# Moving the gathered expert sums from VectorE to GpSimd, half of them into the way down, with three smaller moves

## The chip, the cores and the metric

The kernel runs on one NeuronCore of a Trainium2 chip. Five engines work side by side, each through its own queue, in order: TensorE (PE; its weight loads are listed apart as PEld), VectorE (DVE), ScalarE (ACT), GpSimd (POOL) and SyncE (SP), which only issues DMAs. ACT and POOL issue DMAs too. The metric is device microseconds (us) of one execution; lower is better.

## The reference

Two transformer-like blocks on 512 tokens of width 1024, in float32. What the change touches is the PEER layer of the first block and the S5 layer of the second. PEER scores 128 x 128 product keys, keeps 16 of 16,384 experts in each of 8 heads for every token, and sums the chosen experts, each of which is one row of `expert_down` and one of `expert_up`:

```
u = expert_down[ib]                                  # the way down
act = gelu(einsum("td,thkd->thk", hb, u))
v = expert_up[ib]                                    # the way up
out = einsum("thk,thkd->td", gb * act, v)
```

S5 is a grouped, complex, diagonal state space layer: per group a product into the state, a scan over time, a product out of it, then gelu and two products (GLU) over all channels.

## The kernel before, in words

The tokens stand in the columns of a matrix, channels in the partitions. A product is made of three matmuls (`mm3`, L126 to L128): weights are split into `hi` (ACT, L118) and `lo` (DVE, L119), activations likewise, and hi by hi, hi by lo and lo by hi are added up. Weights come as 128x1024 tiles by SP's queue into `raw`; `raw`, `hi` and `lo` have three buffers each.

PEER treats 416 tokens (TD) densely: all 16,384 experts, 128 at a time, j = 0 to 127. The way down multiplies each tile of `expert_down` with all these tokens, takes gelu, and writes pairs of j as `act_d` (L823 to L825). Beside it, `select` finds the 16 best, and `scatter` writes the gates of the 416 tokens as a dense matrix `g_d` (one-hot matmuls at L745; the DMA to DRAM at L749 is issued by POOL). The way up reads `act_d` (tile `aj`) and, for eight j at a time, `g_d` (tile `gt`) by ACT's queue, multiplies them to `wg` (DVE, L1077), splits `wg` to `wh` (ACT) and `wl` (DVE), and adds up with the tiles of `expert_up` in eight PSUM banks.

The other 96 tokens (TG) go by gathers: 64 tokens on two partitions each and 32 on four (`GROUPS`), in 64 + 32 gathers of 128 rows. POOL issues each as an indirect DMA (L756) into one of three `row` buffers. For `expert_down`, DVE forms the dot products with the tokens (`dot`, L764); for `expert_up`, DVE adds gate x row to `tsum` (`add`, L777 for the first and L779). There are 96 dots and 96 sums; 16 of the sums (`NOW`) stand on the way down, 80 on the way up. 16 PE matmuls per group fold `tsum` into the result (L1097).

What fills the time beside the dense experts is a list of closures with a cost each (`fill`): every j takes as many as its share `per` allows. A scheduler with a timeline of its own then sets the order in each engine's queue; `soon()` raises the priority of the loads, splits and `wg`, and `issue_after` keeps an instruction behind another one.

On the way up the list also holds the preparation of S5's matrices (`s5_prepare`; its input `s5in` is loaded from j = 3 on; results go to DRAM as `mats_d`, by POOL's queue). In the S5 stage later, `u_proj` writes u to DRAM and reads it back in another shape as `u4` (eight DMAs for each of eight m, L1397), `tables(m)` builds the matrices of four pairs (L1406 to L1434), `carry(gi)` the states (L1444 on), `answer(gi)` the outputs (L1478 on). In between stand the products `gate_proj`, `u_proj` and `gla_out` (moving operand `A` for the first two, `B` for the last). Gelu of S5's output then feeds GLU, again with moving operand `A`.

Of the kernel before, what the change touches and what calls it, by code (L numbers as in the profile page):

```python
# [7 lines left out]
F32 = mybir.dt.float32  # L8
# [51 lines left out]
def tile_blocks(ctx, tc, I, out):  # L60
# [500 lines left out]
    with tc.tile_pool(name="peert", bufs=2, reuse_waits="tile") as pt, tc.tile_pool(name="peer", bufs=1, reuse_waits="tile") as pe:  # L561
# [210 lines left out]
        def add(g, i):  # L772
            raw = fetch(I["eu"], g, i)
            w = ggate[g][:, i : i + 1]
            if i == 0:
                tsum[g] = gx.tile([P, D], F32, tag=f"tok{g}", name=f"tsum{g}")
                nc.vector.tensor_scalar(tsum[g], raw, w, None, ALU.mult)  # L777
            else:
                nc.vector.scalar_tensor_tensor(tsum[g], raw, w, tsum[g], ALU.mult, ALU.add)  # L779

        def later(fn):
            with tc.issue_after(low[0].ins):
                fn()

        dot_of = lambda p: (1.4, lambda p=p: dot(*p))
        adds = [(1.3, lambda p=p: later(lambda: add(*p))) for p in picks]


        SPILL, NOW = 0, 16
# [8 lines left out]
        dotted = []  # L798
        for g, (_, n, _) in enumerate(GROUPS):
            dotted += [dot_of(p) for p in picks if p[0] == g]  # L800
            dotted.append((0.1, lambda g=g: weigh(g)))
        cut = len(dotted) - SPILL - 1 if SPILL else len(dotted)
        down, left = dotted[:cut], dotted[cut:]
        down += adds[:NOW]
# [9 lines left out]
        fill.extend(down)  # L814

        per = sum(c for c, _ in fill) / (P - 8)
        done[0] = 0.0
        for j in range(P):
            ps = psum("w")
            linear(ps, I["ed"][j], (hh, hl), TD, TG)  # L820
            if j % 2 == 0:
                at_ = px.tile([P, 2, TD], F32, tag="act", name=nm("at_"))
            nc.scalar.activation(at_[:, j % 2], ps[:, :TD], AF.Gelu)  # L823
            if j % 2 == 1:
                nc.scalar.dma_start(act_d[j // 2], at_.rearrange("p a t -> p (a t)"))  # L825
            run_fill(min((j + 1) * per - done[0], 4.2))
# [199 lines left out]
    with tc.tile_pool(name="s5p", bufs=1, reuse_waits="tile") as s5p, tc.tile_pool(name="up", bufs=2, reuse_waits="tile") as pu:  # L1026
# [6 lines left out]
        def beside():  # L1033
# [7 lines left out]
            of_first = GROUPS[0][1]  # L1041
            gathers = []
            for i, a in enumerate(adds[NOW:of_first]):
                gathers.append(a)
                if left and i % 2 == 1:
                    gathers.append(left.pop(0))
            gathers += left + adds[max(of_first, NOW) :]
# [325 lines left out]
    with tc.tile_pool(name="s5a", bufs=2, reuse_waits="tile") as sp:  # L1373
# [7 lines left out]
        def u_proj(m):  # L1381
# [352 lines left out]
```

## Time and profile before

| | |
|---|---|
| time, median of 3 runs | 2742.34 us (2730.85 to 2746.29) |
| the profiled execution's own time | 2736.44 us |
| span of its profile | 2734.7 us |
| PE busy | 2630.8 us, 96% |
| DVE / ACT / POOL busy | 1874.4 (69%) / 1070.8 (39%) / 491.1 us (18%) |
| the way down ends, the way up begins | about 1103 us, 1107 us |
| the way up's last matmuls, S5's last answer | about 1728 us, 2200 us |

The span is what lies between the first and the last instruction; 1.7 us lie around it. PE's busy share counts modelled matmul ends, so whether a stretch is full is read from how many matmuls it holds. Where PE waits, the profile names the engine that released it. A DMA-issuing instruction stands under the queue's name (SPq, ACTq) and takes no engine time, save on POOL, which makes the descriptors itself.

### The profile page before, as it was taken

To read this page: it belongs to the slowest core of one execution; us is meant where nothing else is said; L and a number is where in the kernel's file an instruction comes from. 1 tells how busy PE (TensorE), PEld (TensorE's weight loads), DVE (VectorE), ACT (ScalarE), POOL (GpSimd) and SP (SyncE) were. 2 spreads that over 40 slices of the span, in tenths; PEclk is the share of its full clock that TensorE was granted. 3 is DMA by queue.
4 is the path that set the end of the run, shared out by engine and by line. 5 is a ranking of instruction groups with operands and counts; after the bars stand their busy time and mean duration, and the time that the engine had idled before them with its cause. 6 is when DMAs were issued, how large, how long until landed. Compare 5 with 4: busy or idle time off the path is not lost.

```text
span 2734.7 us, 36390 instructions
## 1 busy us (share of the span) xinstructions
PE 2630.8 (96%) x13784; PEld 2349.5 (86%) x13784; DVE 1874.4 (69%) x3430; ACT 1070.8 (39%) x1510; POOL 491.1 (18%) x431
## 2 busy tenths in 40 slices
PE   6999999999999999999999899999999989999997
PEld 5777789999999999999899899877788878688886
DVE  5777699998998874788688576744456654562543
ACT  4564333434445444334433233544323243432221
POOL 0001000343343021224423120100002320010100
PEclk9999999999999999999999999999999999999999
DMA  6324424889888577979887887222265654233321
GB/s 255 101 87 139 144 93 133 282 286 327 301 307 323 188 263 259 313 273 339 297 319 265 281 302 258 82 63 70 70 193 177 191 159 132 72 98 96 97 96 66
DMA packets 182304, 532.95 MB, mean 195 GB/s; under 512 B 20592, under 2 KB 59472, under 8 KB 180208
## 3 DMA queue, kind: packets, MB, share of 16 engines
q1 hardware_dynamic: 89872, 282.57, 31.2%
q0 software_dynamic: 39952, 157.64, 16.5%
q10 hardware_dynamic: 52304, 90.41, 9.7%
q8 instruction: 108, 1.77, 0.3%
q14 instruction: 68, 0.56, 0.1%
HBM read 448.98 MB, written 80.41 MB: 194 GB/s over the span
## 4 chain that ended last, share of the span: by engine, by line
PE 84%; DMA 6%; DVE 5%; issue 2%; ACT 2%; POOL 1%; ACTq 0%; SPq 0%; DVEq 0%; POOLq 0%
PE ps L127 24%; PE ps L126 24%; PE ps L128 24%; PE ps L745 4%; DMA gt<-g_d 3%; DMA row<-in_eu_dram,gid 1%; DVE lo L119 1%; PE ps L1307 1%; PE ps L1310 1%; DVE wg L1077 1%; PE ps L615 1%; PE ps L148 0%; PE ps L1421 0%; ACT hi L118 0%; PE ps L487 0%
## 5 line engine op out<-in xcount | busy, mean ns | idle before, releaser
L118 ACT ACTIVATE hi<-raw 128x1024 fp32r<-128x1024 f32 (+2 forms) x459 | 481.3, 1051 | 1068.0 <-PE ps L127 796.9
L119 DVE TENSOR_TENSOR lo<-raw,hi 128x1024 fp32r<-128x1024 f32 (+2 forms) x459 | 579.4, 1264 | 347.6 <-ACT hi L118 319.1
L126 PE MATMUL ps<-h2h,hi 128*128 128x416 f32 (+1 forms) x1152 | 413.1, 360 | 3.9 <-ACT h2h L569 3.0
L127 PE MATMUL ps<-h2l,hi 128*128 128x416 f32 (+1 forms) x1152 | 413.1, 359 | 2.9 <-DVE h2l L570 2.9
L128 PE MATMUL ps<-h2h,lo 128*128 128x416 f32 (+1 forms) x1152 | 411.2, 358 | 0.0
L127 PE MATMUL ps<-wl,hi 128*128 128x416 f32 x1024 | 363.8, 355 | 11.4 <-DVE wl L132 11.4
L128 PE MATMUL ps<-wh,lo 128*128 128x416 f32 x1024 | 358.4, 357 | 10.9 <-DVE lo L119 10.9
L126 PE MATMUL ps<-wh,hi 128*128 128x416 f32 x1024 | 351.2, 355 | 6.6 <-ACT wh L131 4.5
L126 PE MATMUL ps<-Ah,hi 128*128 128x512 f32 (+2 forms) x944 | 337.7, 363 | 18.0 <-ACT Ah L131 7.0
L127 PE MATMUL ps<-Al,hi 128*128 128x512 f32 (+2 forms) x944 | 340.6, 361 | 2.7 <-DVE Al L1123 2.7
L128 PE MATMUL ps<-Ah,lo 128*128 128x512 f32 (+2 forms) x944 | 338.1, 359 | 0.5 <-DVE lo L119 0.5
L756 POOL DMA_INDIRECT row<-in_eu_dram,gid x96 | 181.9, 1895 | 398.5 <-DVE tsum L779 329.6
L126 PEld LDWEIGHTS ps<-h2h,hi 128*128 128x128 f32 x1152 | 218.0, 189 | 11.5 <-ACT h2h L569 3.8
L127 PEld LDWEIGHTS ps<-h2l,hi 128*128 128x128 f32 x1152 | 217.8, 189 | 9.9 <-DVE h2l L570 3.6
L128 PEld LDWEIGHTS ps<-h2h,lo 128*128 128x128 f32 x1152 | 217.8, 189 | 6.4
L126 PEld LDWEIGHTS ps<-Ah,hi 128*128 128x128 f32 x944 | 179.0, 191 | 50.0 <-ACT Ah L131 7.9
L127 PEld LDWEIGHTS ps<-wl,hi 128*128 128x128 f32 x1024 | 194.4, 190 | 16.6 <-DVE wl L132 13.0
L127 PEld LDWEIGHTS ps<-Al,hi 128*128 128x128 f32 x944 | 180.2, 191 | 32.6 <-issue 5.0
L128 PEld LDWEIGHTS ps<-wh,lo 128*128 128x128 f32 x1024 | 195.5, 191 | 13.1 <-DVE lo L119 11.9
L128 PEld LDWEIGHTS ps<-Ah,lo 128*128 128x128 f32 x944 | 179.6, 190 | 30.7 <-issue 6.0
L126 PEld LDWEIGHTS ps<-wh,hi 128*128 128x128 f32 x1024 | 196.0, 192 | 10.2 <-ACT wh L131 5.2
L756 POOL DMA_INDIRECT row<-in_ed_r_dram,gid x96 | 144.6, 1506 | 218.9 <-DVE dots L764 194.1
(602 smaller groups left out, 4199.5 us busy)
## 6 DMA issues: line engine op xcount, KB each, us to landing
raw<-in_ed_dram SPq DMA_DIRECT2D x128, 512.0 KB, 5.1
raw<-in_eu_dram SPq DMA_DIRECT2D x128, 512.0 KB, 5.5
raw<-in_win_dram SPq DMA_DIRECT2D x67, 512.0 KB, 3.6
raw<-in_wff_dram SPq DMA_DIRECT2D x64, 512.0 KB, 3.8
g_d<-gst POOLq DMA_DIRECT2D x13, 2048.0 KB, 9.7
aj<-act_d ACTq DMA_DIRECT2D x64, 416.0 KB, 4.5
wa<-in_wada_dram SPq DMA_DIRECT2D x46, 512.0 KB, 4.5
gt<-g_d ACTq DMA_DIRECT2D x45, 512.0 KB, 9.8
```

Of the source, the lines that this page charges most:

```text
L118: top[0] = nc.scalar.activation(hi[:, :n], raw[:, :n], AF.Copy)
L119: low[0] = nc.vector.tensor_sub(lo[:, :n], raw[:, :n], hi[:, :n].bitcast(F32))
L126: nc.tensor.matmul(ps, wh, x[0], start=first, stop=False)
L127: nc.tensor.matmul(ps, wh, x[1], start=False, stop=False)
L128: nc.tensor.matmul(ps, wl, x[0], start=False, stop=last)
L615: nc.tensor.matmul(ps[:, t * P : t * P + P], q[:, t * P : t * P + P], skt[:, m], start=True, stop=True)
L745: nc.tensor.matmul(ps[:, i * P : i * P + P], o1[:, c, :, i], o2[a][:, c, :, i], start=a == 0, stop=a == 1)
L756: nc.gpsimd.indirect_dma_start(out=raw, out_offset=None, in_=src.rearrange("a b d -> (a b) d"), in_offset=bass.IndirectOffsetOnAxis(ap=gid ...
L1077: nc.vector.tensor_tensor(wg.rearrange("p (c t) -> p c t", t=TC), aj[:, j % 2].rearrange("p (c t) -> p c t", t=TC), gt[:, :, j % 8], ALU.mult)
L1307: nc.tensor.matmul(po[hs], qx[:, c * 64 : c * 64 + 64], st, start=False, stop=True)
L1310: nc.tensor.matmul(ps, kt[hs, j], vt[hs, j], start=True, stop=True)
```

## The change

Four edits. First, all 96 sums move from DVE to POOL. A sum is now two instructions, gate x row in place (`tensor_scalar`, with the first one of a group writing `tsum`) and `tsum` + row (`tensor_tensor`). They are issued one gather behind on the way down (lag 1) and two behind on the way up. 48 sums instead of 16 are in the way down's list: 32 in turn with the 32 dots of the second group, 16 at the list's end. Second, `aj` for j = 0 and 1 goes to two buffers of another tag, by SP's queue, and `gt` is issued behind `hi` of j - 8 instead of j - 6. Third, the read-back of `u4` is issued by POOL instead of SP. Fourth, `tables(m + 1)` is written behind `carry(gi + 1)` instead of ahead of it.

```diff
-        def add(g, i):
-            raw = fetch(I["eu"], g, i)
-            w = ggate[g][:, i : i + 1]
-            if i == 0:
-                tsum[g] = gx.tile([P, D], F32, tag=f"tok{g}", name=f"tsum{g}")
-                nc.vector.tensor_scalar(tsum[g], raw, w, None, ALU.mult)
-            else:
-                nc.vector.scalar_tensor_tensor(tsum[g], raw, w, tsum[g], ALU.mult, ALU.add)
+        pending = []
+        def sums_of(lag):
+            while len(pending) > lag:
+                g, i, raw = pending.pop(0)
+                w = ggate[g][:, i : i + 1]
+                if g not in tsum:
+                    tsum[g] = gx.tile([P, D], F32, tag=f"tok{g}", name=f"tsum{g}")
+                    nc.gpsimd.tensor_scalar(tsum[g], raw, w, None, ALU.mult)
+                else:
+                    nc.gpsimd.tensor_scalar(raw, raw, w, None, ALU.mult)
+                    nc.gpsimd.tensor_tensor(tsum[g], tsum[g], raw, ALU.add)
+        def add(g, i, lag):
+            pending.append((g, i, fetch(I["eu"], g, i)))
+            sums_of(lag)
...
-        SPILL, NOW = 0, 16
+        NOW, LAST = 48, 16
...
+        down = [dot_of(p) for p in picks[:n0]] + [(0.1, lambda: weigh(0))]
+        dots_, adds_ = [dot_of(p) for p in picks[n0:]], adds[: NOW - LAST]
+        while dots_ or adds_:
+            for l in (dots_, adds_):
+                if l:
+                    down.append(l.pop(0))
...
-        fill.extend(down)
-        per = sum(c for c, _ in fill) / (P - 8)
+        fill.extend(down + adds[NOW - LAST : NOW] + [(0.1, lambda: sums_of(0))])
+        per = sum(c for c, _ in fill) / (P - 6)
...
-            run_fill(min((j + 1) * per - done[0], 4.2))
+            run_fill(min((j + 1) * per - done[0], 4.8))
...
-                with tc.issue_after(tops[max(j - 6, 0)].ins) if j else ExitStack():
+                with tc.issue_after(tops[max(j - 8, 0)].ins) if j else ExitStack():
...
+                if j == 0:
+                    aj = [tp.tile([P, TD], F32, tag="tl", name=nm("aj"), bufs=3) for _ in range(2)]
+                    for i, a in enumerate(aj):
+                        nc.sync.dma_start(a, act_d[0][:, i * TD : i * TD + TD])
...
-                        nc.sync.dma_start(u4[r0 : r0 + 16, 4 * m : 4 * m + 4], usrc[g, s])
+                        nc.gpsimd.dma_start(u4[r0 : r0 + 16, 4 * m : 4 * m + 4], usrc[g, s])
...
-            if gi % 2 == 0 and gi + 2 < NGR:
-                nxt = tables(gi // 2 + 1)
             if gi % 2 == 1:
                 sts = nxt
             cur, held = held, carry(gi + 1, sts) if gi + 1 < NGR else None
+            if gi % 2 == 0 and gi + 2 < NGR:
+                nxt = tables(gi // 2 + 1)
```

POOL's queue in the middle of the way down, at the first gathers of the second group (`gid_2365`; `in_ed_r` rows are for dots, `in_eu` rows for sums). Before:

```order
L756 DMA row_7204<-in_ed_r_dram,gid_2361 128x1024
L756 DMA row_7243<-in_ed_r_dram,gid_2365 128x1024
L756 DMA row_7309<-in_ed_r_dram,gid_2365 128x1024
L756 DMA row_7407<-in_ed_r_dram,gid_2365 128x1024
L756 DMA row_7411<-in_ed_r_dram,gid_2365 128x1024
```

Now:

```order
L756 DMA row_6770<-in_ed_r_dram,gid_2365 128x1024
L756 DMA row_6869<-in_eu_dram,gid_2361 128x1024
L756 DMA row_6871<-in_ed_r_dram,gid_2365 128x1024
L756 DMA row_6937<-in_eu_dram,gid_2361 128x1024
L781 TENSOR_SCALAR tsum_6939<-row_6869,ggate_2362 128x1024
L783 TENSOR_SCALAR row_6937<-row_6937,ggate_2362 128x1024
L756 DMA row_7002<-in_ed_r_dram,gid_2365 128x1024
L756 DMA row_7039<-in_eu_dram,gid_2361 128x1024
L784 TENSOR_TENSOR tsum_6939<-tsum_6939,row_6937 128x1024
L756 DMA row_7104<-in_ed_r_dram,gid_2365 128x1024
L783 TENSOR_SCALAR row_7039<-row_7039,ggate_2362 128x1024
```

Each gather for a dot now has a gather for a sum and the two instructions of an earlier sum around it in the same queue. Later in this queue 34 of the 48 sums stand ahead of the two memsets of S5's preparation (L957), and the other 14 behind them and behind the DMA `mats_d<-s5in`, which waits for an input that is loaded on the way up.

The issue of one `gt` on ACT and its first use on DVE, at j = 98 of the way up. Before, ACT and then DVE:

```order
L118 ACTIVATE hi_14288<-raw_14287 128x1024
L1067 DMA gt_14528<-g_d 128x4x256
L119 TENSOR_TENSOR lo_14289<-raw_14287,hi_14288 128x1024
L132 TENSOR_TENSOR wl_14295<-wg_14293,wh_14294 128x416
L119 TENSOR_TENSOR lo_14325<-raw_14323,hi_14324 128x1024
L779 SCALAR_TENSOR_TENSOR tsum_13340<-row_14359,ggate_2366,tsum_13340 128x1024
L132 TENSOR_TENSOR wl_14331<-wg_14329,wh_14330 128x416
L1077 TENSOR_TENSOR wg_14541<-aj_14533,gt_14528 128x416
```

Now, at j = 96, ACT and then DVE:

```order
L118 ACTIVATE hi_14321<-raw_14320 128x1024
L1068 DMA gt_14626<-g_d 128x4x256
L119 TENSOR_TENSOR lo_14322<-raw_14320,hi_14321 128x1024
L132 TENSOR_TENSOR wl_14328<-wg_14326,wh_14327 128x416
L119 TENSOR_TENSOR lo_14358<-raw_14356,hi_14357 128x1024
L132 TENSOR_TENSOR wl_14364<-wg_14362,wh_14363 128x416
L1084 TENSOR_TENSOR wg_14639<-aj_14631,gt_14626 128x416
```

The issue moved two j ahead, and the first `wg` that reads the tile moved with it: in both one further `lo` lies between.

PE's queue at S5's last answer. Before:

```order
L1480 MATMUL ps_19546<-s5xi_19537,em_19426 128x128
L126 MATMUL ps_19969<-Ah_19633,hi_19971 128x512
L126 MATMUL ps_20005<-Ah_19633,hi_20007 128x512
L126 MATMUL ps_20043<-Ah_19633,hi_20045 128x512
L127 MATMUL ps_19969<-Al_19634,hi_19971 128x512
```

Now:

```order
L1487 MATMUL ps_19642<-s5xi_19633,em_19522 128x128
L128 MATMUL ps_19781<-Bh_15648,lo_19784 128x512
L126 MATMUL ps_19781<-Bh_15648,hi_19783 128x512
L127 MATMUL ps_19781<-Bl_15649,hi_19783 128x512
L128 MATMUL ps_19781<-Bh_15648,lo_19784 128x512
```

Before, GLU (`Ah_19633`, made by gelu from S5's output) came right behind the last answer; now 175 matmuls of `gla_out` (`Bh_15648`) come first. In exchange 417 instead of 489 of the three-matmul products stand between the first carry and the last answer; the first two answers have few between them.

## Rows read from the trace of the kernel before

**Rows 1.** Windows: length; busy PE, PEld, DVE, ACT, POOL (instructions); clock, DMA share, GB/s.

```profile
500.00:1050.00 550.00, 549.13 (x3213) 530.71 (x3212) 476.63 (x736) 256.32 (x318) 175.99 (x123) 1.00 0.82 288
1100.00:1150.00 50.00, 45.68 (x231) 44.73 (x230) 36.26 (x93) 17.88 (x25) 11.05 (x5) 0.93 0.91 307
1150.00:1700.00 550.00, 525.38 (x2727) 515.64 (x2726) 425.48 (x677) 190.57 (x260) 163.75 (x92) 0.98 0.86 296
1250.00:1300.00 50.00, 50.00 (x267) 49.46 (x266) 43.28 (x59) 21.51 (x30) 24.74 (x12) 1.00 0.97 348
1500.00:1600.00 100.00, 88.38 (x449) 85.97 (x448) 59.94 (x86) 28.71 (x39) 20.63 (x13) 0.95 0.87 284
```

**Rows 2.** What PE waited for, 1100 to 1730: us in total, times, longest.

```profile
PE ps L127 <- DVE wl L132: 11.4, 4, 4.0
PE ps L128 <- DVE lo L119: 10.9, 3, 8.8
```

**Rows 3.** Chain that ended last, at the turn: start us, us, what.

```profile
1095.53 7.34 DMA act_d<-at__1440_9905
1102.90 3.03 DMA aj<-act_d
```

**Rows 4.** The chain on the way up, two of its DMAs.

```profile
1486.52 14.16 DMA gt<-g_d
...
1519.59 27.26 DMA row<-in_eu_dram,gid
```

**Rows 5.** DVE by line, 1100 to 1730: count | busy us, mean ns | idle before, releasers.

```profile
L779 DVE SCALAR_TENSOR_TENSOR tsum<-row,ggate,tsum 128x1024 f32<-128x1024 f32 x79 | 100.9, 1278 | 15.9 <-DMA row<-in_eu_dram,gid 15.9
L1077 DVE TENSOR_TENSOR wg<-aj,gt 128x416 f32<-128x416 f32 x128 | 70.2, 584 | 55.7 <-DMA gt<-g_d 36.9 <-DMA aj<-act_d 9.5 <-issue 9.2
```

**Rows 6.** S5: windows at its end.

```profile
2200.00:2220.00 20.00, 13.04 (x57) 10.13 (x56) 7.83 (x14) 10.62 (x13) 9.64 (x19) 0.78 0.62 187
2220.00:2240.00 20.00, 19.45 (x82) 15.38 (x81) 8.50 (x12) 11.78 (x15) 0.00 (x0) 0.97 0.37 113
2240.00:2260.00 20.00, 20.00 (x90) 16.57 (x89) 11.21 (x14) 6.82 (x9) 0.00 (x0) 1.00 0.54 171
```

**Rows 7.** S5: what PE waited for, 2000 to 2240.

```profile
PE ps L126 <- ACT Ah L131: 7.0, 2, 3.5
PE ps L126 <- ACT hi L118: 4.3, 1, 4.3
```

**Rows 8.** S5: SP's queue, the read-back of u in one go.

```profile
1990.54 21.45 SPq L1397 DMA_DIRECT2D u<-u_d  x40
```

**Rows 9.** Timeline in the last stage: POOL, then DVE beside and without it.

```profile
2443.21 1.04 POOL L1591 TENSOR_TENSOR f<-f 128x512 f32<-128x512 f32 x1 [4.40 <-ACT hi L118]
...
2443.24 2.09 DVE L119 TENSOR_TENSOR lo<-raw,hi 128x1024 fp32r<-128x1024 f32 x1 [0.18 <-ACT hi L118]
...
2465.18 1.23 DVE L119 TENSOR_TENSOR lo<-raw,hi 128x1024 fp32r<-128x1024 f32 x1 [4.24 <-ACT hi L118]
```

**Rows 10.** POOL by line, whole span: a memset of 128x1024.

```profile
L950 POOL MEMSET bd<- 128x1024 f32 x2 | 1.9, 984 | 0.0
```

**Rows 11.** Windows around the moved sums.

```profile
750.00:900.00 150.00, 149.50 (x885) 143.34 (x885) 131.69 (x205) 69.02 (x86) 54.38 (x39) 1.00 0.87 306
900.00:1104.00 204.00, 202.86 (x1184) 197.93 (x1182) 133.24 (x168) 93.43 (x117) 29.06 (x23) 1.00 0.68 239
1100.00:1200.00 100.00, 95.68 (x496) 94.23 (x495) 78.76 (x190) 34.39 (x47) 22.39 (x11) 0.97 0.86 296
```

**Rows 12.** POOL's timeline at the start of the way up.

```profile
1123.64 1.72 POOL L976 DMA_DIRECT2D mats_d<-s5in  x1 [56.99 <-DMA s5in<-in_s_dram]
```

**Rows 13.** The page, part 5: POOL's gathers for the dots.

```profile
L756 POOL DMA_INDIRECT row<-in_ed_r_dram,gid x96 | 144.6, 1506 | 218.9 <-DVE dots L764 194.1
```

**Rows 14.** DMA issues, 765 to 890: gathers for the dots, count, median us to landing.

```profile
row<-in_ed_r_dram,gid POOLq DMA_INDIRECT x29, 6.9
```

**Rows 15.** DVE by line, 420 to 1104: the dots.

```profile
L764 DVE CUSTOM_DVE_ANT_0 junk<-row,htok 128x1024 bf16<-128x1024 f32 x96 | 116.0, 1218 | 21.4 <-DMA row<-in_ed_r_dram,gid 21.3
```

More of the change, by code (lines that the diff above doesn't have):

```diff
@@ L770, in tile_blocks @@
         tsum = {}
-        def add(g, i):
-            raw = fetch(I["eu"], g, i)
-            w = ggate[g][:, i : i + 1]
-            if i == 0:
-                tsum[g] = gx.tile([P, D], F32, tag=f"tok{g}", name=f"tsum{g}")
-                nc.vector.tensor_scalar(tsum[g], raw, w, None, ALU.mult)
-            else:
-                nc.vector.scalar_tensor_tensor(tsum[g], raw, w, tsum[g], ALU.mult, ALU.add)
-        def later(fn):
-            with tc.issue_after(low[0].ins):
-                fn()
+        pending = []
[12 more added lines that the diff above has]
+            sums_of(lag)
         dot_of = lambda p: (1.4, lambda p=p: dot(*p))
-        adds = [(1.3, lambda p=p: later(lambda: add(*p))) for p in picks]
-        SPILL, NOW = 0, 16
+        NOW, LAST = 48, 16
+        adds = [(1.3, lambda p=p, n=n: add(*p, 1 if n < NOW else 2)) for n, p in enumerate(picks)]
         select(0)
@@ L797, in tile_blocks @@
         todo, fill[:] = fill[:], []
[L798 to L804, printed above, removed]
+        n0 = GROUPS[0][1]
+        down = [dot_of(p) for p in picks[:n0]] + [(0.1, lambda: weigh(0))]
[4 more added lines that the diff above has]
+                    down.append(l.pop(0))
+        down += [(0.1, lambda g=g: weigh(g)) for g in range(1, len(GROUPS))]
         share = sum(c for c, _ in down) / sum(c for c, _ in todo)
@@ L1040, in beside @@
             fill.clear()
[L1041 to L1047, printed above, removed]
+            gathers = adds[NOW:] + [(0.1, lambda: sums_of(0))]
             share = sum(c for c, _ in gathers) / sum(c for c, _ in rest)
@@ L1068, in tile_blocks @@
             if j % 2 == 0:
-                aj = px.tile([P, 2, TD], F32, tag="act", name=nm("aj"))
-                nc.scalar.dma_start(aj.rearrange("p a t -> p (a t)"), act_d[j // 2])
+                if j == 0:
+                    aj = [tp.tile([P, TD], F32, tag="tl", name=nm("aj"), bufs=3) for _ in range(2)]
+                    for i, a in enumerate(aj):
+                        nc.sync.dma_start(a, act_d[0][:, i * TD : i * TD + TD])
+                else:
+                    at_ = px.tile([P, 2, TD], F32, tag="act", name=nm("aj"))
+                    nc.scalar.dma_start(at_.rearrange("p a t -> p (a t)"), act_d[j // 2])
+                    aj = [at_[:, i] for i in range(2)]
             w = load_w(I["eu"][j])
@@ L1077, in tile_blocks @@
                 nc.vector.tensor_tensor(
-                    wg.rearrange("p (c t) -> p c t", t=TC), aj[:, j % 2].rearrange("p (c t) -> p c t", t=TC), gt[:, :, j % 8], ALU.mult)
+                    wg.rearrange("p (c t) -> p c t", t=TC), aj[j % 2].rearrange("p (c t) -> p c t", t=TC), gt[:, :, j % 8], ALU.mult)
                 split(wg, wh, wl)
```

## The prediction

> **What bounds the kernel now.** I started from TensorE, since it is busy nearly all the time, and asked stretch by stretch how many matmuls it holds against a clean one. A clean 50 us of the way up holds 267 at clock 1.00 [rows 1], so one costs 0.1873 us and the 24 of one tile 4.48 us. Between 500 and 1050 us the way down has PE busy for 549.13 of 550 us at clock 1.00: nothing can be won there, only lost. Between 1150 and 1700 us, 11 x 267 = 2937 would fit and 2727 stand there: 210 x 0.1873 = 39 us are lost, 24.6 as idle time, the rest as a granted clock of 0.98, which falls behind gaps (0.95 in the worst 100 us).
>
> Next, what ends PE's waits. On the way up it is DVE: `wl` 11.4 us, `lo` 10.9 us, one of these 8.8 us long [rows 2]. DVE itself is not full (425.48 of 550 us). The views of its lines and of the chain say what it waits for: a `gt` load (36.9 us ahead of `wg`, against 14.16 us that one such load takes on the chain) and a gathered row (15.9 us ahead of the sum, against a landing of 27.26 us) [rows 4, 5]. Since DVE works in order, a sum without its row holds up the `lo` behind it. The 100 us from 1500 with that row hold 449 of 534 matmuls: 85 x 0.1873 = 15.9 us.
>
> At the turn the chain goes through the write of the last `act_d` (7.34 us) and the read of the first `aj` (3.03 us) [rows 3]; 1100 to 1150 us holds 231 of 267, so 6.7 us are lost. At the end of S5, PE waits 7.0 us for `Ah` (gelu before GLU) and earlier 4.3 us for a `hi` [rows 7]. Beside that `hi`, SP's queue issues the 40 DMAs of `u4` for 21.45 us [rows 8], with weight loads behind them. The 40 us around the tail hold 57 + 82 matmuls where the clean 20 us after them hold 90 [rows 6]: 41 x 0.222 = 9.1 us.
>
> **The change part by part**, against the profiled execution's 2736.44 us (5.9 below the median of the runs).
>
> *First activations in own buffers, by SP: -6.* They no longer wait for a turn of the way down's buffers; the write before them stays on the path. Ends: -6.7 (the whole loss) and 0 (the write alone sets the end, or SP's weight loads stand ahead). As `gt` for j = 0 is there by then, I take nearly all.
>
> *Sums off DVE, the waits for rows: -12.* A late row now stops POOL alone. Ends: -15.9 and 0; not all, since a late row also comes from a full DMA (0.87 busy in that stretch), which delays weights as well.
>
> *`gt` issued two j earlier: -3.* The first use moves along in the order, with one `lo` in between as before; the load gets no more lead. What helps is that 32 gathers of 0.5 MB leave the way up. The way up's loss beyond the row is 39 - 15.9 = 23 us, most of it `gt`: ends -10 (half of it goes) and +5.
>
> *S5: -8.* The 175 `gla_out` matmuls at the tail are worth 175 x 0.22 = 39 us of work and cover the 7.0 us for `Ah` with its clock: -9.1. `u4` on POOL frees SP: -4.3; POOL has little else then. Against it, those matmuls are gone from between the answers: 417 products where 489 stood, few beside the first two answers, where PE may wait for `carry`: +5 taken, ends 0 and +12.
>
> *The sums on POOL.* The trace has no such instruction. The addition of 128x512 took 1.04 us [rows 9], so 1024 columns take 2 x 1.04 = 2.08. For the scaling the nearest rows are a memset of that size, 0.984 us [rows 10], and the addition, 2.08; I take 1.0, nearer the memset since one operand is read. A sum is 3.1 us of POOL (3.0 to 4.1) against 1.28 on DVE [rows 5].
>
> What it does to DVE shows in rows 9: `lo` took 2.09 us when it began beside a POOL addition and 1.23 alone, so 0.86 more of 1.04. A DVE instruction with two inputs waits for nearly the whole POOL instruction. Taken in full, every sum holds DVE for up to 3.1 us, so the move gives DVE no time; it takes away its waits in order.
>
> The Trainium skill (*SBUF — State Buffer*, Who interferes with whom) says the same: DVE and GpSimd share a port pair, which the first to issue holds for its whole instruction, and a DVE instruction with two SBUF inputs contends with a GpSimd one that reads. The trace agrees (0.86 of 1.04 us). By that rule taken for every sum, DVE would be blocked for 96 x 3.1 = 298 us, where it worked 96 x 1.28 = 123 us before; that speaks against this change.
>
> *Way down: +8.* 34 sums come to it ahead of the memsets; of its 16 before, some 15 that cost 1.28 leave DVE (79 more stand on the way up [rows 5]). From 750 to 1104 us DVE worked 131.69 + 133.24 = 264.9 us [rows 11]. Less 15 x 1.28 = 19 and plus 34 x 3.1 = 105 that is 351 of 354 us: full on the mean, if every hold is paid. The first 150 us hold most of the pairs. There 29 dots landed in 125 us [rows 14], 4.3 us for a listed cost of 1.4; a pair of 1.4 + 1.3 takes 8.3 us, so 15 pairs stand in their place: 131.7 + 15 x 3.1 - 14 x 1.22 [rows 15] = 161, so 11 over; three buffers of `lo` hold 3 x 4.48 = 13.4 us. A part falls into DVE's waits and one-input work, so I take +8. Ends 0 and +35; the upper end is these 11 us with 34 x 0.7 = 24 by which a scaling of 1.7 us instead of 1.0 would lengthen the sums.
>
> *Start of the way up: +6.* 14 sums stand behind `mats_d<-s5in`, which came at 1123.64 after 56.99 us of waiting [rows 12]; POOL then does them in a row: 43 us. With DVE's 78.76 us from 1100 to 1200 less ten sums of 1.28 that makes 109 of 100 us: 9 over, +6 taken, ends 0 and +25. From there on it is 425.5 - 88 (79 x 550/630 = 69 sums) + 48 x 3.1 = 486 of 550 us; a hold is shorter than the buffers' 13.4 us, so I take nothing more.
>
> Sum: -6 - 12 - 3 - 8 + 8 + 6 = -15, so 2721.4; I forecast 2722.
>
> **Rivals.**
>
> *Slower: POOL's queue becomes a loop on the way down.* POOL waits long already, 194.1 us for dots that free `row` buffers [rows 13]. Now the gathers for dots stand behind the additions of sums in the same in-order queue, three buffers for both. A gather lands 6.9 us after issue [rows 14], the dot takes 1.2 us [rows 15], the addition ahead of the next gather 2.08: 10.2 us a pair, if they follow one another. The place has 8.3 us for a pair, as worked out above. Then 32 x 1.9 = 61 us late; DVE in order waits in its dots, and PE behind `lo`. Less the buffers' 13 that is 48 in place of 8: 2736.4 - 29 + 48 + 6 = 2761. It decides from 8.3 us a pair on. For it: DVE waits 21.3 us for dots' rows even now. Against it: with three buffers two gathers can be under way, which halves the landing's share: 6.9 / 2 + 3.3 = 6.8 us.
>
> *Faster still: the holds cost nothing.* If they fall into DVE's free time (23% of 1150 to 1700, 25% of 750 to 1104) and all waits go: -6.7 - 15.9 - 10 - 13.4 (S5 without its new gap) = -46, so 2690. For it: DVE is ahead of PE by up to three tiles, and PE waited for nothing in the way down. Against it: 351 of 354 us.
>
> *About the same: the next wait is as late.* With the row gone, weights and `gt` come over the same DMA at 0.87 busy; `wg` still waits its 36.9 us, and PE's gap moves from `lo` to `wl`. Sums -4, gathers' relief 0: -6 - 4 - 0 - 8 + 8 + 6 = -4, so 2732. For it: `wl` cost PE as much as `lo` [rows 2]. Against: the 8.8 us gap is the longest, and it hangs on the row.
>
> That the change doesn't do what it says holds in part: of 48 sums for the way down, 34 are done there, which is in the terms.
>
> **How the numbers follow.** My forecast's case 0.4 (own range 2704 to 2734), the slower rival 0.2 (2745 to 2780), the faster 0.2 (2685 to 2704), the same 0.2 (2724 to 2745). About 0.5% or 14 us is what a measurement tells from no change: faster is below 2728.6, slower above 2756. Faster: 0.3 of the forecast, 0.2 of the faster rival and 0.08 of the third, 0.58. Slower: most of the loop, 0.16, and 0.02 of the unknown scaling, 0.18. The rest, 0.24, is the same. The range 2694 to 2760 leaves out under half of the fast rival and about half of the slow one.
>
> **What would show it.** Per step: in the way down, matmuls of 750 to 1104 us against 885 + 1184 (8 us are 43 fewer), the mean of `lo` above 1.23 us, and POOL's scaling and addition near 1.0 and 2.08 us. At the turn, 260 or more matmuls in 1100 to 1150 us and no `aj` in the chain. On the way up, no DVE wait for `row` and no gap of 8 us behind `lo`, while `wg` still waits for `gt` (over 25 us). POOL waits at `mats_d<-s5in`, then 14 sums in a row. At S5's end no wait for `Ah`; at its start some us for `carry`. Wrong would make me: additions well over 2.08 us; pairs over 8.3 us, with gaps in DVE at the dots; or a `lo` that doesn't lengthen beside POOL, and then the faster rival.

## The result and the profile after

The changed kernel takes 2857.24 us (median of 4 runs, 2847.92 to 2859.84) against 2741.35 us before on the same chip: a ratio of 1.0422, 95% interval 1.0383 to 1.0461. The forecast was 2722 us, the range 2694 to 2760. It is slower by 4.2%, well beyond the range and on the other side.

First the windows of the changed kernel that answer to those of before [rows 1, 11]. Columns: stretch, its length, busy PE, PEld, DVE, ACT, POOL (instructions), granted clock, DMA share, GB/s.

```profile
500.00:1050.00 550.00, 534.46 (x3103) 514.37 (x3103) 510.22 (x699) 248.30 (x304) 321.21 (x173) 0.98 0.80 281
1150.00:1700.00 550.00, 463.81 (x2272) 444.45 (x2271) 459.32 (x566) 161.14 (x223) 386.19 (x181) 0.92 0.74 243
750.00:900.00 150.00, 142.58 (x839) 135.29 (x838) 145.98 (x198) 71.65 (x88) 106.63 (x50) 0.97 0.74 260
900.00:1104.00 204.00, 197.98 (x1140) 193.12 (x1140) 165.57 (x149) 85.22 (x107) 163.49 (x80) 0.98 0.78 278
1200.00:1250.00 50.00, 38.69 (x176) 36.21 (x175) 48.62 (x60) 9.97 (x14) 47.19 (x20) 0.90 0.67 223
1250.00:1300.00 50.00, 50.00 (x266) 49.44 (x265) 37.22 (x47) 19.53 (x27) 10.77 (x6) 1.00 0.71 224
1650.00:1700.00 50.00, 47.26 (x249) 46.08 (x247) 33.24 (x28) 12.88 (x17) 44.35 (x20) 1.00 0.75 254
```

The way down, full before, has lost 90 matmuls from 750 to 1104 us (1979 against 2069), 15 us at what one cost there before (354 us for 2069). The way up holds 2272 matmuls in 550 us where 2727 stood. In it, the loss stands where POOL is dense: the 50 us with POOL at 10.77 us hold 266 matmuls, as many as a clean stretch; those with POOL at 47.19 us hold 176, and DVE, with only 60 instructions, is busy for 48.62 us of them. The last row is a warning: POOL at 44.35 us again, but DVE has 28 instructions and is busy for two thirds of the time, and 249 matmuls go through. By these rows it takes both, a busy POOL and much work on DVE.

What DVE and POOL do there, by line. Columns: line, engine, operation, tiles, shapes, count | busy us, mean ns | idle before, releasers. DVE on the way up, first two lines of before (1104 to 1730 us; `wg` stands in [rows 5]):

```profile
L119 DVE TENSOR_TENSOR lo<-raw,hi 128x1024 fp32r<-128x1024 f32 x128 | 156.3, 1222 | 54.4 <-ACT hi L118 46.6 <-PE ps L127 5.0 <-DMA raw<-in_eu_dram 2.4
L132 DVE TENSOR_TENSOR wl<-wg,wh 128x416 fp32r<-128x416 f32 x128 | 74.6, 584 | 19.5 <-ACT wh L131 19.4
```

Now, from 1104 to 1845 us:

```profile
L119 DVE TENSOR_TENSOR lo<-raw,hi 128x1024 fp32r<-128x1024 f32 x132 | 191.1, 1449 | 83.3 <-ACT hi L118 83.2
L132 DVE TENSOR_TENSOR wl<-wg,wh 128x416 fp32r<-128x416 f32 x128 | 116.2, 909 | 4.9 <-ACT wh L131 4.6
L1084 DVE TENSOR_TENSOR wg<-aj,gt 128x416 f32<-128x416 f32 x128 | 104.8, 841 | 52.4 <-DMA gt<-g_d 37.2 <-DMA aj<-act_d 8.6 <-issue 5.5
```

And POOL's sums:

```profile
L783 POOL TENSOR_SCALAR row<-row,ggate 128x1024 f32<-128x1024 f32 x94 | 299.4, 3185 | 40.4 <-DMA row<-in_eu_dram,gid 38.9
L784 POOL TENSOR_TENSOR tsum<-tsum,row 128x1024 f32<-128x1024 f32 x94 | 238.0, 2532 | 2.7
```

A sum takes 3.19 + 2.53 = 5.7 us of POOL, not 3.1. In a quiet stretch each part takes little more than the shortest of its 94 (2.84 and 2.34 us), as in the first two rows of this timeline (start us, us, engine, line, operation):

```profile
1068.95 2.86 POOL L783 TENSOR_SCALAR row<-row,ggate 128x1024 f32<-128x1024 f32 x1
1071.89 2.41 POOL L784 TENSOR_TENSOR tsum<-tsum,row 128x1024 f32<-128x1024 f32 x1
...
1208.30 4.10 DVE L883 TENSOR_TENSOR s_er<-s_t,s_t 128x32 f32<-128x32 f32 x1
1208.84 2.43 POOL L784 TENSOR_TENSOR tsum<-tsum,row 128x1024 f32<-128x1024 f32 x1
```

The last two rows show a hold: a DVE instruction on 128x32, of a kind that took 0.2 us in the kernel before, takes 4.10 us here. POOL's addition lies wholly within it; the remaining 1.5 us or so fall beside a gather's issue before the addition and a scaling behind it. DVE shows as busy meanwhile: held time is counted as its own. So `lo` went from 1222 to 1449 ns, `wg` from 584 to 841 [rows 5], `wl` from 584 to 909.

PE's waits on the way up answer to [rows 2]; three waits of ACT and POOL stand with them. Columns: who, for whom: us in total, times, longest.

```profile
ACT hi L118 <- DVE wg L1084: 200.4, 27, 21.2
PE ps L127 <- DVE wl L132: 76.9, 30, 11.4
POOL mats_d L992 <- ACT bd L990: 65.0, 8, 39.3
POOL mats_d L1015 <- DVE bd L884: 42.1, 1, 42.1
PE ps L126 <- ACT wh L131: 17.0, 4, 9.6
PE ps L128 <- DVE lo L119: 3.5, 4, 1.5
```

The wait for `lo` behind a gathered row is gone, as forecast (10.9 to 3.5 us, and POOL, not DVE, now waits for rows); that for `wl` went from 11.4 to 76.9 us. The first row was 50.9 us before. It shows one way by which a hold reaches the weights too: ACT's queue is in order, so while `wh` waits for a held `wg`, the `hi` behind it waits as well.

At the turn from the way down to the way up the chain that ended last goes through POOL's queue (start us, us, what):

```profile
1093.46 2.68 POOL tsum L784
1096.29 1.81 POOL row L756
...
1106.10 6.57 DMA row<-in_ed_r_dram,gid
1112.70 2.81 DVE junk L764
...
1119.83 9.26 DMA gt<-g_d
```

The gather at 1096.29 stands behind a scaling and an addition in POOL's queue. The next one, at 1106.10, waits for the dot that frees its buffer. So the last dot comes at 1112.7 us, and ACT waits for it (the row below) with loads of `gt` behind it in its queue:

```profile
ACT dots L767 <- DVE dots L764: 10.6, 1, 10.6
```

The 32 dots that have sums between them start 11.3 us apart on the mean, from 762.8 to 1112.7 us; before, without sums between, 3.8 us apart. DVE's wait for dots' rows from 740 to 1104 us rose with it. Before, then now:

```profile
L764 DVE CUSTOM_DVE_ANT_0 junk<-row,htok 128x1024 bf16<-128x1024 f32 x37 | 44.7, 1219 | 7.3 <-DMA row<-in_ed_r_dram,gid 7.2
L764 DVE CUSTOM_DVE_ANT_0 junk<-row,htok 128x1024 bf16<-128x1024 f32 x35 | 51.5, 1473 | 28.1 <-DMA row<-in_ed_r_dram,gid 28.1
```

Over the whole span, the same 3334 DVE instructions were busy for 1781.0 us in the run e1_short below and for 2030.4 us here: 249 us of holds.

### The profile page after: what moved, and what is told of

Its sections match the earlier page's. It is cut to its first block, busy times and chain, and to the rows that moved or that the text cites. A ratio compares the mean times of both kernels' runs of the same rounds, so it can differ in the third digit from the quotient of the medians.

```text
span 2846.1 us, 36363 instructions
## 1 busy us (share of the span) xinstructions
PE 2658.9 (93%) x13784; PEld 2365.2 (83%) x13784; DVE 2030.4 (71%) x3334; ACT 1070.3 (38%) x1510; POOL 1006.6 (35%) x685
## 4 chain that ended last, share of the span: by engine, by line
PE 64%; DVE 19%; DMA 7%; issue 6%; POOL 2%; ACT 2%; ACTq 1%; SPq 0%; DVEq 0%; POOLq 0%
PE ps L127 18%; PE ps L126 18%; PE ps L128 18%; DVE lo L119 5%; DMA gt<-g_d 3%; DVE wg L1084 2%; PE ps L745 2%; DVE wl L132 2%; DVE o L740 1%; DMA row<-in_ed_r_dram,gid 1%; POOL row L783 1%; DVE oh L734 1%; ACT hi L118 1%; PE ps L1314 1%; POOL row L756 1%
## 5 line engine op out<-in xcount | busy, mean ns | idle before, releaser
L119 DVE TENSOR_TENSOR lo<-raw,hi 128x1024 fp32r<-128x1024 f32 (+2 forms) x459 | 634.0, 1383 | 342.0 <-ACT hi L118 327.5
L127 PE MATMUL ps<-wl,hi 128*128 128x416 f32 x1024 | 376.8, 368 | 77.1 <-DVE wl L132 76.9
L126 PE MATMUL ps<-wh,hi 128*128 128x416 f32 x1024 | 367.0, 364 | 22.0 <-ACT wh L131 17.0
L128 PE MATMUL ps<-wh,lo 128*128 128x416 f32 x1024 | 373.1, 365 | 2.9 <-DVE lo L119 2.9
L783 POOL TENSOR_SCALAR row<-row,ggate 128x1024 f32<-128x1024 f32 x94 | 299.4, 3185 | 40.4 <-DMA row<-in_eu_dram,gid 38.9
L127 PEld LDWEIGHTS ps<-wl,hi 128*128 128x128 f32 x1024 | 201.6, 197 | 92.7 <-DVE wl L132 88.6
L784 POOL TENSOR_TENSOR tsum<-tsum,row 128x1024 f32<-128x1024 f32 x94 | 238.0, 2532 | 2.7
L128 PEld LDWEIGHTS ps<-h2h,lo 128*128 128x128 f32 x1152 | 219.0, 190 | 10.9 <-DVE lo L119 4.5
L126 PEld LDWEIGHTS ps<-wh,hi 128*128 128x128 f32 x1024 | 202.7, 198 | 27.0 <-ACT wh L131 18.4
L128 PEld LDWEIGHTS ps<-wh,lo 128*128 128x128 f32 x1024 | 202.0, 197 | 5.9 <-DVE lo L119 4.2
```

The source lines that it names most:

```text
L119: low[0] = nc.vector.tensor_sub(lo[:, :n], raw[:, :n], hi[:, :n].bitcast(F32))
L126: nc.tensor.matmul(ps, wh, x[0], start=first, stop=False)
L127: nc.tensor.matmul(ps, wh, x[1], start=False, stop=False)
L128: nc.tensor.matmul(ps, wl, x[0], start=False, stop=last)
L783: nc.gpsimd.tensor_scalar(raw, raw, w, None, ALU.mult)
L784: nc.gpsimd.tensor_tensor(tsum[g], tsum[g], raw, ALU.add)
```

## The experiments

Each ratio is against the kernel before on the same chip (2738.39 to 2740.90 us). Three marks divide every run's profile: the first matmul that uses `wl` (the turn), the first that folds `tsum` (the way up's end), and the end of the span.

| kernel | turn, us | way up, us | behind it, us |
|---|---|---|---|
| before | 1110.1 | 608.4 | 1016.2 |
| after | 1134.9 | 706.4 | 1004.8 |
| e1_short | 1112.0 | 594.9 | 1002.6 |
| e2_write | 1117.8 | 660.0 | 1005.1 |
| e3_dve | 1119.4 | 592.2 | 1003.8 |
| e4_three | 1103.3 | 612.1 | 1003.4 |
| e5_act | 1126.7 | 651.2 | 1004.5 |
| e6_places | 1116.2 | 726.6 | 1005.0 |
| e7_split | 1179.5 | 667.5 | 1052.5 |
| e8_dve32 | 1121.9 | 601.3 | 1004.4 |
| e9_u4 | 1113.4 | 604.3 | 1003.5 |
| e10_late48 | 1115.4 | 610.4 | 1004.1 |
| e11_late32 | 1105.9 | 599.6 | 1003.1 |
| e12_late40 | 1110.1 | 590.5 | 1003.4 |

The kernels before and e9_u4 have the same instructions in the same order on PE, DVE, ACT and POOL up to 1690 us, and their turns and ways up differ by 3.3 and 4.1 us; differences of that size between two rows say nothing.

The theory: POOL's sums hold DVE, and PE pays. The rivals: POOL's in-order queue of gathers; the 48 sums' place on the way down; or losses in the three smaller moves.

### e1_short: the sums cut to 64 columns

```diff
-                    nc.gpsimd.tensor_scalar(raw, raw, w, None, ALU.mult)
-                    nc.gpsimd.tensor_tensor(tsum[g], tsum[g], raw, ALU.add)
+                    nc.gpsimd.tensor_scalar(raw[:, :64], raw[:, :64], w, None, ALU.mult)
+                    nc.gpsimd.tensor_tensor(tsum[g][:, :64], tsum[g][:, :64], raw[:, :64], ALU.add)
```

> Left out: 15/16 of every sum (scaling and addition on POOL touch 64 of the 1024 columns; the two first ones of a group stay whole). Gathers, queues, waits and the number of instructions stay as in the changed kernel (2857 us). Theory (holds): the 94 sums take 5.7 us of POOL each and shut out DVE's two-input instructions meanwhile; cut to some 0.3 us each the loss goes: 2720 to 2750 us, mean of lo on the way up 1.25 us against 1.45. Rival (queue): the gathers for dots and sums wait for one another in POOL's in-order queue with three buffers, whatever the sums take: 2820 us or more.

Measured: 2715.33 us, ratio 0.9911 (0.9881 to 0.9941). With every gather, queue and wait in place and only the sums' length gone, the whole loss is gone. A queue with short sums in it costs nothing. This alone does not part the holds from a queue that long sums slow down: the 32 dots with sums between them are 8.2 us apart here and 11.3 in the changed kernel. e2_write and e6_places below do more of that. The run also bounds the idea: sums that cost DVE next to nothing bring the way up from 608.4 to 594.9 us here. What POOL still did, in place of 3185 and 2532 ns:

```profile
L783 POOL TENSOR_SCALAR row<-row,ggate 128x64 f32<-128x64 f32 x94 | 77.0, 819 | 60.6 <-DMA row<-in_eu_dram,gid 58.3
L784 POOL TENSOR_TENSOR tsum<-tsum,row 128x64 f32<-128x64 f32 x94 | 51.4, 547 | 7.3
```

### e2_write: POOL as busy, but only writing

```diff
-                    nc.gpsimd.tensor_scalar(raw, raw, w, None, ALU.mult)
-                    nc.gpsimd.tensor_tensor(tsum[g], tsum[g], raw, ALU.add)
+                    for _ in range(3):
+                        nc.gpsimd.memset(raw, 0.0)
+                    nc.gpsimd.memset(tsum[g], 0.0)
+                    nc.gpsimd.memset(tsum[g], 0.0)
+                    nc.gpsimd.memset(tsum[g][:, : D // 2], 0.0)
```

> Left out: the sums; in the place of each, memsets of the same buffers keep POOL busy about as long (3 + 2.5 memsets of 128x1024 at 0.95 to 0.98 us, some 5.3 us), but read nothing. Theory (holds, by the reading side): DVE is not held though POOL is as busy: 2720 to 2760 us, lo near 1.25 us. Rival 1 (holds by any POOL work, reads or not): 2830 to 2860. Rival 2 (POOL's queue is too slow with 5.3 us a sum, without any hold): 2790 or more, with lo at 1.25 us and DVE waiting for rows.

Measured: 2776.67 us, ratio 1.0139 (1.0077 to 1.0201): above the range for the theory, below those of its rivals. DVE by line and shape, from 1104 to 1850 us:

```profile
L119 DVE TENSOR_TENSOR lo<-raw,hi 128x1024 fp32r<-128x1024 f32 x138 | 170.4, 1236 | 125.5 <-ACT hi L118 125.0 <-PE ps L128 0.3
L1008 DVE COPY s_pvr<-s5e 128x32 f32<-128x32 f32 x8 | 29.4, 3679 | 0.0
L896 DVE TENSOR_SCALAR s_pt<-s_pt 128x32 f32<-128x32 f32 x8 | 18.1, 2258 | 0.2
```

`lo`, with two inputs, is hardly held any more (1236 ns against 1222), `wg` and `wl` a little (670 and 623 against 584). But small instructions with one input now are: the copy takes 192 ns in the kernel before and 3679 here on the mean, longer than any single memset, so that it waits for several in a row. Two sides are held by two kinds of POOL work. The Trainium skill (*SBUF — State Buffer*, Who interferes with whom) states both: an instruction with two inputs contends with POOL's reads and not with a mere write, and copies and `tensor_scalar` can enter modes that take the whole shared pair of ports. `lo` and the copy agree with it. The expectation knew the first half alone.

On the way down the run comes near to a slow queue without holds: POOL is busy for 302 us from 750 to 1104 (270 in the changed kernel), DVE for 249.7 us as in e1_short (251.0; the changed kernel 311.6). The dots with sums between them are 9.5 us apart, DVE waits 27.4 us for dots' rows, and the turn is 5.8 us later than in e1_short. On the way up, where no dot waits, 87.7 us more of DVE time come with 65.1 us more of length.

### e3_dve: the sums on DVE, 48 still listed for the way down

```diff
-                    nc.gpsimd.tensor_scalar(raw, raw, w, None, ALU.mult)
-                    nc.gpsimd.tensor_tensor(tsum[g], tsum[g], raw, ALU.add)
+                    nc.vector.scalar_tensor_tensor(tsum[g], raw, w, tsum[g], ALU.mult, ALU.add)
```

(and the first sum of a group likewise)

> The changed kernel with every sum as one instruction on DVE again, 48 of them still on the way down, lags kept. Theory (holds): DVE pays 1.28 us a sum and no hold: 2725 to 2765 us. Rival (placement: 48 sums and their gathers on the way down are the loss, whoever adds): 2820 us or more. That the way down gets 32 more sums of 1.28 us on DVE (41 us in 354, with 90 us free there) should cost under 15 us by either.

Measured: 2716.85 us, ratio 0.9918 (0.9892 to 0.9944): faster than expected by either. More sums and gathers on the way down make no loss where DVE adds them. Without the constraint that kept a sum behind the latest `lo`, 54 sums stand ahead of the way up in DVE's queue, and 42 are left for it. The turn is late, though: on ACT's queue the write of an `act_d` could not be issued at once (before: 0.52 us).

```profile
1095.98 7.14 ACTq L831 DMA_DIRECT2D act_d<-at__1472_10001  x1
```

### e4_three: only the three smaller moves

The diff is that of the change without its first edit.

> The kernel before with the three smaller moves alone (first activations in own buffers, gt two j earlier, the two S5 edits); sums as before. From the terms of the prediction -6 -3 -8 = -17: 2724 us; the changed kernel's time from the end of the way up on is already 11 us shorter than before. Rival (the three moves are worth nothing by themselves): 2736 to 2746 us.

Measured: 2722.26 us, ratio 0.9942 (0.9923 to 0.9961). The sum of the three terms is right. Their parts are not: behind the way up 12.8 us are won, the turn is 6.8 us earlier, and the way up 3.7 us longer, which is within what two equal kernels differ by.

### e5_act: ACT scales, POOL adds

```diff
-                    nc.gpsimd.tensor_scalar(raw, raw, w, None, ALU.mult)
+                    nc.scalar.activation(raw, raw, AF.Copy, scale=w)
                     nc.gpsimd.tensor_tensor(tsum[g], tsum[g], raw, ALU.add)
```

> The changed kernel with the scaling (2.86 us on POOL when undisturbed) made by ACT; POOL keeps the addition (2.40 us), in the same places. Theory (the loss goes with the time POOL holds the way shared with DVE): 2.4 of 5.26 us are left, so 2715 + 142 x 0.46 = 2780 us, 2755 to 2800. Rival (the number of POOL instructions or any POOL addition at all does it): 2830 or more. Rival 2 (only above a full DVE does the hold cost, so half of it costs little): 2735 or less. What ACT takes on, 96 x about 1.1 us in 1100 us, at 40% busy, should not show.

Measured: 2785.46 us, ratio 1.0156 (1.0135 to 1.0177), as the theory has it. This run is the one that judges the prediction's step: POOL's sums take less here (2.59 us, 243 us in all) than the 3.1 us and 298 us that the prediction reckoned with, and still cost 70 us over e1_short. Not all of that need be holds: ACT does 48 scalings on the way up, and its in-order queue waits at them 24.4 us for `wg` and 14.0 us for rows there. The run does not part this from the holds.

```profile
L784 POOL TENSOR_TENSOR tsum<-tsum,row 128x1024 f32<-128x1024 f32 x94 | 243.4, 2590 | 135.9 <-ACT row L783 134.2
```

### e6_places: all sums on POOL, 16 listed for the way down as before

```diff
-        NOW, LAST = 48, 16
+        NOW, LAST = 16, 16
```

> The changed kernel with 16 sums on the way down, at its end, and 80 on the way up, as before; all 96 still on POOL. Theory (holds): 32 x 5.3 us of holds move from the way down to the way up, where PE already waits for wl: 2850 to 2900 us. Rival (the way down's pairs of gathers in POOL's queue are the loss): 2760 to 2820 us.

Measured: 2851.28 us, ratio 1.0393 (1.0368 to 1.0418), in the theory's range, but not for its reason. The edit moved far fewer than 32 sums: 26 are done before the turn, where the changed kernel has 32. What it did was to take the sums out from between the dots: the last dot comes at 879 us (882 before), and not at 1112.7. The turn is 18.7 us earlier, so the pairs in POOL's queue do cost the turn, as the rival has it, though they are not the whole loss. The way up is 20.2 us longer with 6 sums more on it and DVE held for 32.7 us more. That the two cancel is chance.

With this run, five kernels have as many DVE instructions (688 or 689) and matmuls (3028 to 3033) on the way up and different holds. The number of POOL's sums there differs as well, from 43 in e1_short to 70 in e6_places; their gathers are not the loss, since the kernel before has 80 sums there in 608.4 us. Each row is the window of that kernel's way up: e1_short, e5_act, e2_write, after, e6_places.

```profile
1112.00:1707.00 595.00, 581.11 (x3032) 570.52 (x3030) 384.76 (x688) 211.83 (x288) 128.74 (x145) 0.99 0.79 266
```
```profile
1127.00:1778.00 651.00, 598.89 (x3031) 584.20 (x3030) 474.23 (x688) 260.74 (x336) 204.62 (x116) 0.95 0.74 248
```
```profile
1118.00:1778.00 660.00, 595.96 (x3033) 582.30 (x3031) 472.43 (x688) 210.45 (x288) 358.17 (x386) 0.94 0.76 252
```
```profile
1135.00:1841.00 706.00, 613.53 (x3029) 590.57 (x3028) 560.24 (x689) 210.53 (x288) 445.00 (x207) 0.93 0.73 240
```
```profile
1116.00:1842.00 726.00, 623.62 (x3028) 599.33 (x3027) 592.99 (x689) 209.96 (x288) 494.69 (x226) 0.92 0.73 239
```

The third busy time (DVE's) and the length behind the stretch rise together. Against e1_short, DVE is held for 89.5, 87.7, 175.5 and 208.2 us, and the way up is longer by 56.3, 65.1, 111.5 and 131.7: 0.63, 0.74, 0.64 and 0.63 us for each us of hold. In the changed kernel some 79 of the 111 us are idle time of PE, and 32 us are matmuls, as many as in e1_short, that take longer at a mean granted clock of 0.93 in place of 0.99 (613.53 against 581.11 us busy). In none is DVE full: in the changed kernel it is idle for 146 of 706 us. No threshold shows between 88 and 208 us of holds.

### e7_split: each POOL instruction in four

```diff
-                    nc.gpsimd.tensor_scalar(raw, raw, w, None, ALU.mult)
-                    nc.gpsimd.tensor_tensor(tsum[g], tsum[g], raw, ALU.add)
+                    for q in range(0, D, 256):
+                        nc.gpsimd.tensor_scalar(raw[:, q : q + 256], raw[:, q : q + 256], w, None, ALU.mult)
+                    for q in range(0, D, 256):
+                        nc.gpsimd.tensor_tensor(tsum[g][:, q : q + 256], tsum[g][:, q : q + 256], raw[:, q : q + 256], ALU.add)
```

> Every scaling and addition of the changed kernel in four of 256 columns (376 more POOL instructions; POOL's sum of time the same or some more). Theory (one instruction holds DVE to its own end, and DVE and POOL take turns): a DVE instruction waits 0.7 instead of 2.9 us, and S5's many small ones lose least: 2740 to 2800 us. Rival (the time that POOL works is what counts): 2850 us or more.

Measured: 2905.81 us, ratio 1.0602 (1.0575 to 1.0629); the expectation fell. Four pieces take 4 x 1333 + 4 x 948 ns = 9.1 us, against 5.7 in one:

```profile
L784 POOL TENSOR_SCALAR row<-row,ggate 128x256 f32<-128x256 f32 x376 | 496.5, 1333 | 41.2 <-DMA row<-in_eu_dram,gid 40.0
L786 POOL TENSOR_TENSOR tsum<-tsum,row 128x256 f32<-128x256 f32 x376 | 347.5, 948 | 1.8
```

POOL then falls behind, and at the end PE waits for the last sum itself:

```profile
PE ps L1106 <- POOL tsum L786: 46.5, 1, 46.5
```

How much of a piece is its own time and how much a wait for DVE this run does not tell, so whether shorter holds would have been cheaper stays open.

### e8_dve32: as e3_dve with 32 listed for the way down

```diff
-        NOW, LAST = 48, 16
+        NOW, LAST = 32, 0
```

> Sums on DVE as in e3_dve (2717 us), 32 instead of 48 on the way down, all in turn with the dots and none at its end. In e3_dve the way up began 16 us later than with the three moves alone, behind a write of act_d that took 13.6 us on a DMA 0.89 busy. Theory (the 16 gathers at the end of the way down crowd that write): the turn gives back 8 to 16 us, 16 sums more on the way up take some: 2700 to 2712 us. Rival (the way up is worth as much per sum): 2714 to 2722.

Measured: 2730.84 us, ratio 0.9968 (0.9954 to 0.9982). It did not test what it was meant to: the scheduler drew sums ahead again, 54 before the turn as in e3_dve. With the same count the two are 14 us apart; in the profiles 9.1 us of it lie on the way up (601.3 against 592.2 us). What makes them was not taken apart.

### e9_u4: only the read-back of u4 on POOL

```diff
-                        nc.sync.dma_start(u4[r0 : r0 + 16, 4 * m : 4 * m + 4], usrc[g, s])
+                        nc.gpsimd.dma_start(u4[r0 : r0 + 16, 4 * m : 4 * m + 4], usrc[g, s])
```

> The kernel before with one edit: the read-back of u4 is issued by POOL instead of SP. All kernels with both S5 edits take 11 to 14 us less than before from the end of the way up on. Theory of the prediction (SP's queue 4.3, the gla_out matmuls behind the last answer 9.1, less 5 for the gap early in S5): this edit alone gives 4 us: 2734 to 2738 against 2740. Rival (the blocked queue of weight loads is the larger part): 2727 to 2731.

Measured: 2722.96 us, ratio 0.9948 (0.9932 to 0.9964): even beyond the rival, and all that the three moves bring together. Behind the way up it has 1003.5 us, e4_three 1003.4, so the other order of the tables adds nothing that shows. Nor is the wait for `Ah` there any more: with this edit alone the trace has 88 matmuls of `gla_out` behind the last answer. The windows that answer to [rows 6], of e9_u4 at its own tail:

```profile
2190.00:2210.00 20.00, 20.00 (x88) 16.20 (x87) 8.34 (x10) 10.04 (x11) 6.43 (x12) 1.00 0.74 249
2210.00:2230.00 20.00, 19.46 (x85) 15.50 (x84) 10.58 (x13) 10.47 (x12) 0.00 (x0) 1.00 0.43 143
```

### e10_late48, e11_late32, e12_late40: DVE's sums kept behind `lo`

```diff
-        adds = [(1.3, lambda p=p, n=n: add(*p, 1 if n < NOW else 2)) for n, p in enumerate(picks)]
+        def later(fn):
+            with tc.issue_after(low[0].ins):
+                fn()
+        adds = [(1.3, lambda p=p, n=n: later(lambda: add(*p, 1 if n < NOW else 2))) for n, p in enumerate(picks)]
```

on e3_dve, with `NOW, LAST` of 48 and 16, 32 and 0, 40 and 0.

> Sums on DVE with the three moves; every sum is again kept behind the latest lo, as before, so that those listed for the way up are not drawn ahead: 47 instead of 54 (e3_dve) stand before the way up. Theory (a full DMA at the turn holds the last act_d): still 16 gathers at the way down's end: turn within 4 us of e3_dve (first wl matmul at 1119 us), 2710 to 2722. Rival (the sums' order against the lo's is what set the way up): below 2708.

> As e10_late48 with 32 sums on the way down, none behind the last dot. Theory (a full DMA at the turn): the last act_d is written in under 8 us, first wl matmul at 1103 to 1109 us, as with the three moves alone; 64 sums stay on the way up (80 there gave 612 us, 42 gave 592): 603 us, so 2708 to 2716. Rival (the turn depends on something else): 2716 to 2726.

> As e11_late32 with 40 sums on the way down, in turn with the dots. Theory: 56 on the way up give 599 us; the turn lies between those of e10_late48 and e11_late32; 2706 to 2718. Rival (order and turn vary by 10 us with every such change, and no count is better): 2716 to 2730.

Measured: 2725.53 us, ratio 0.9948 (0.9930 to 0.9966); 2712.35 us, ratio 0.9906 (0.9885 to 0.9928); 2706.47 us, ratio 0.9887 (0.9863 to 0.9911). e11_late32 and e12_late40 came as expected, the latter the fastest kernel of all and 1.1% under the one before. e10_late48 missed its range by 3.5 us; its turn is as expected, its way up is not (610.4 us with fewer sums on it than in e12_late40). With no gathers at the end of the way down, `act_d` was issued without a stall in e12_late40:

```profile
1098.04 0.52 ACTq L835 DMA_DIRECT2D act_d<-at__1464_9977  x1
```

and its way up is near clean, 3027 matmuls in the 590 us from 1110, with the sums' instructions on DVE:

```profile
1110.00:1700.00 590.00, 579.00 (x3027) 569.39 (x3027) 440.89 (x744) 210.63 (x288) 105.29 (x73) 0.99 0.82 279
```

DVE does 56 more instructions there than in e1_short and is 56 us busier, and the way up is as short. Work in DVE's queue costs nothing that shows here; the smallest added hold measured, 87.7 us in e2_write, cost 65.1 us.

## Why the prediction was wrong, point by point

- **What bounds the kernel: right.** The way down had only to lose, and it lost; the way up hung on DVE.
- **First activations, -6: right at the turn, not in the sum.** In e4_three the turn is 6.8 us earlier than before. Against e9_u4, which lacks this edit and the next, the time is the same (2722.26 and 2722.96 us): what the turn gained the way up gave back.
- **`gt`, -3: nothing that shows.** The wait of `wg` is 37.2 us, as it was (36.9).
- **Rows' waits, -12: right as a mechanism, the size not shown.** DVE waits for no row of a sum on the way up, and e1_short has the way up 13.5 us shorter than before. But e12_late40, with every sum on DVE, has it shorter still (590.5 us).
- **S5, -8: right in sign, a third too small, and wrong in its parts.** 11.4 us in the changed kernel. The queue of SP, mis-sized at 4.3, brings all of it: with it freed, the order changes as well and covers the wait for `Ah`. The +5 for a gap at `carry` did not come: PE waits for nothing over 2.1 us from 1960 to 2320.
- **A sum's price, 3.1 us (3.0 to 4.1): mis-sized.** 5.7 us, or 2.86 + 2.41 undisturbed. The addition was estimated fairly from [rows 9] (2.08), the scaling was read off a memset [rows 10], which reads nothing: 0.98 against 2.86 us. The other end named there, the addition, was the nearer one.
- **The holds: right, and not too small.** DVE's added time, 249 us, lies below the 298 us that the prediction put as the full price.
- **What the holds cost on the way up: the step that failed.** "a hold is shorter than the buffers' 13.4 us, so I take nothing more", and +6 for the start. Against e1_short the changed kernel has its way up 111.5 us longer, far beyond the ends of 0 and +25. DVE's free time, read as a mean over a stretch, is not free: `wg`, `wh`, `wl` follow one another across DVE and ACT before every tile, and both queues are in order. PE's waits for `wl` and `wh` there are 93.9 us, for `lo` 3.5: the buffers of `lo`, on which the prediction leaned, are not where PE stopped. 0.63 us of each held us came out at the end. By that rate and the prediction's own 298 us the loss would have been 188 us, not 14. e5_act, with sums cheaper than predicted, shows that the right price alone would hardly have saved the forecast.
- **Way down, +8 (0 to +35): inside its ends, too small.** The turn is 22.9 us later than in e1_short. Holds and the loop of gathers both stand there: DVE is busy for 60.5 us more from 750 to 1104 us, and the dots with sums between them are 11.3 us apart where the prediction had room for 8.3. How the 22.9 us split is open. The sign of "43 fewer" matmuls for 8 us took the way up's 0.1873 us; at the way down's 0.171 it is 47, and 90 were missing.
- **The slower rival, 2761 us: its mechanism came, beside the larger one.** It reckoned 10.2 us a pair with a sum's addition alone; 11.3 were measured, and the turn's chain runs through POOL's queue as it says. e6_places, without the pairs, has the turn 18.7 us earlier. e1_short does not speak against it, since its short sums make the pairs 8.2 us. But it had nothing for the way up, where most of the loss is.
- **That the sums' move is worth having at all:** no run bears it out. e12_late40 has PE's wait for `lo` gone too, with all sums on DVE; from e4_three (2722 us) it differs by 24 gathers and sums more on the way down, not by less work on DVE.

Open: why the way up differs by 10 to 20 us among e3_dve, e8_dve32, e10_late48 and e12_late40, all with their sums on DVE; and whether the bunching of sums behind POOL's waits for `mats_d` (65.0 and 42.1 us) makes the holds dearer. Neither was taken apart.

## What to carry to other kernels

Before moving elementwise work to GpSimd, ask what it holds on VectorE, and price each us of hold as mostly lost (0.63 to 0.74 us here) where VectorE stands in a chain that feeds TensorE tile by tile; a mean of idle time on VectorE is no cover. Ask too what stands behind the moved work in GpSimd's in-order queue: here it was the gathers that another stage waited for. Price an operation by one that reads and writes as it does, never by a memset. A DMA queue blocked by many small issues is cheap to free, and here that one line, with 40 of the sums taken earlier on their old engine, was the gain.

## What the runs showed of the hardware

- On POOL, scaling 128x1024 in place by a column took 2.84 us at the least, longer than adding two such tiles (2.34), though it reads one tile fewer.
- Beside memsets on POOL a one-input copy of 128x32 on DVE took 3.7 us on the mean (192 ns in the kernel before), while `lo`, with two inputs, took 1236 ns against 1222.
- On the way up DVE was held for 87.7 to 208.2 us more than in e1_short, and the way up was longer by 0.63 to 0.74 us for each.
- Four pieces of 256 columns take 9.1 us on POOL where whole instructions take 5.7.
